# Seven half products in place of eight for the output projection of a hybrid streaming encoder layer

## The chip, the cores and the metric

The kernel runs on one core of a Trainium2 chip. The metric is the device time of one execution in microseconds, as the median of several runs of the same program. Beside the timed runs there is one profiled execution; all rows of the trace come from it. TensorE does the matmuls and writes them to PSUM, VectorE (DVE), ScalarE (ACT) and GpSimd (POOL) do the elementwise work, and SyncE (SP) issues most of the DMAs. GpSimd can't read PSUM.

## What is computed

The layer has 1152 tokens: 1024 of a prompt and 8 times 16 of running streams. It forms a normalised input, one combined input projection of 6664 columns, a matrix-memory branch (mLSTM) and a banded attention branch, and joins them. Only the last part is touched here:

```python
def merge_out(x, h_m, mz, h_a, az, gm, ga, w_bm, w_ba, w_out):
    u_m = jnp.einsum("btc,cd->btd", h_m * jax.nn.silu(mz), w_bm)
    u_a = jnp.einsum("btc,cd->btd", h_a * jax.nn.silu(az), w_ba)
    mix = jax.nn.sigmoid(gm) * u_m + jax.nn.sigmoid(ga) * u_a
    return x + jnp.einsum("btd,de->bte", mix, w_out)
```

Here `h_m` and `h_a` have 512 channels, `mix` and the result 1024. All is float32.

## The kernel before

Everything is held transposed: channels on the 128 partitions, tokens along the columns. A float32 product is made of three fast ones. `split` (L118 to L121) writes a value as a high part (a ScalarE copy to the type fp32r, L120) and a low part (the difference, L121, on VectorE unless GpSimd is named), and `mm3` (L123 to L126) multiplies high by high, high by low and low by high into one PSUM bank. Weights go the same way: a raw tile of 512 columns is loaded (`wr`), and `w_halves` makes `wh` and `wl` of it; `wpA` has three raw buffers and four of each half.

The stages are: input norm; value columns; twelve jobs of the input projection (`chunk_of`, L445 for the matmuls); mLSTM; attention; branch projection of the attention; output projection. The twelve jobs already use a scheme of seven products for eight. There a pair of column tiles is multiplied with sums of quarters of `h` (two halves of the 1024 channels by two halves of the 1152 tokens), which `quarter_sums` (L274 to L289) had formed for 64 tokens at a time, with six VectorE and six GpSimd operations of 4 x 64 columns a call. GpSimd forms the differences of the raw weights (L424).

The last two stages run after the attention, in the function `emit` from L1162 on:

- The last step of the attention writes its outputs to DRAM (`o_sc`), and `load_ops(o_sc, 4)` (L1086) reads them back in pieces of 288 tokens by two tiles and splits them into `h2`. The branch projection of the mLSTM (`um_work`, evacuated at L1098) ran before that, on `h1` and `h21`.
- Branch projection of the attention: eight tiles j, each in three chunks of 384 tokens, 4 x 3 matmuls a chunk. `ev_a` takes a chunk: VectorE multiplies it with the gate (L1174, reads PSUM), GpSimd adds the part of the mLSTM, `sm` (L1175), and `split` writes it to `x_hi` and `x_lo`. `sm` and the gate `ta` come from DRAM, one DMA each of 1152 tokens per j, two sets of buffers.
- Output projection: eight tiles e, each in three chunks of 384 tokens, 8 x 3 matmuls a chunk over the eight tiles of x. The evacuation (L1188) adds the residual x (`xr`, loaded at L1187), and a DMA on ScalarE's queue stores it (L1189).

PSUM has six banks for both stages, taken in turn. The order of the instructions on each engine and queue is fixed when the program is built: a planner simulates the program with costs of its own, and an engine is given the earliest instruction in the text that is ready when it comes free; on the chip each engine then runs that order and waits by semaphores. So loads of the last stage can stand ahead of others (`xr` is issued by SP at 929.8 us). A buffer that lies over one of a closed pool waits until that one has been read for the last time.

Of the kernel before, what the change touches and what calls it, by code (L numbers as in the profile page):

```python
# [32 lines left out]
def emit(tc, a, o, ctx):  # L33
# [4 lines left out]
    def open_pool(name, bufs=1, side=None, space=None):  # L38
        es = ExitStack()
        kw = {"name": name, "bufs": bufs, "reuse_waits": "tile"}  # L40
        if side:
            kw["side"] = side
        if space is not None:
            kw["space"] = space
        return es, es.enter_context(tc.tile_pool(**kw))

    def keep(*args, **kw):
        es, p = open_pool(*args, **kw)
        ctx.enter_context(es)
        return p  # L50
# [54 lines left out]


    h1 = [hp.tile([P, KH, HF], F32R, name=f"h1_{q}") for q in ("hi", "lo")]
    h2 = [hp.tile([P, KH, T], F32R, name=f"h2_{q}") for q in ("hi", "lo")]

    def hcols(k, c0, c1):  # L110

# [1054 lines left out]
    for j in range(8):
        sa = fp.tile([P, 2 * T], F32, tag="sa", name="sa")
        sm, ta = sa[:, 0:T], sa[:, T:2 * T]
        sp.dma_start(sm, sm_sc[j])
        sp.dma_start(ta, tg_sc[8 + j])  # L1170
# [7 lines left out]
        feature_tile(load_nt(a["wba"][j], 4), lambda k, c: hcols(4 + k, c * CH, (c + 1) * CH), ev_a, 4, pp, "pu")  # L1178

    def x_rhs(k, c):  # L1180
        s = slice(c * CH, (c + 1) * CH)
        return x_hi[:, k, s], x_lo[:, k, s]

    for e in range(8):
        def ev(c, ps):
            xr = stg.tile([P, CH], F32, tag="wqr", name="xr", bufs=4).rearrange("p (i t) -> p i t", i=3)
            sp.dma_start(xr, a["xT"][3 * c:3 * c + 3, :, e, :].rearrange("i p t -> p i t"))  # L1187
            dve.scalar_tensor_tensor(out=xr, in0=ps.rearrange("p (i t) -> p i t", i=3), scalar=0.5, in1=xr, op0=ALU.mult, op1=ALU.add)  # L1188
            act.dma_start(o["y"][e][:, c * CH:(c + 1) * CH], xr.rearrange("p i t -> p (i t)"))  # L1189

        feature_tile(load_nt(a["wout"][e]), x_rhs, ev, KD, pp, "pu")
    esPS.close()
    esF.close()

def layout(x):
# [105 lines left out]
```

## Time and profile before

| what | value |
|---|---|
| median of three runs | 1103.8 us (1100.98 to 1110.57) |
| profiled execution | 1099.79 us, its span 1098.0 us |
| TensorE, VectorE, ScalarE, GpSimd busy | 1045.6, 661.7, 529.3, 457.9 us |
| mean granted TensorE clock | 0.989 |
| TensorE's share of the chain that ended last | 62% |

The span runs from the first to the last instruction; the execution has 1.8 us around it. A matmul's recorded duration overlaps with its neighbours', so its price in a dense stretch is the stretch by the number of matmuls. PEld is the loading of weights into TensorE, which overlaps with the matmuls. The branch projection of the attention takes about 937.7 to 992.5 us of the span, the output projection 992.5 to 1094.7.

### The profile page before, as it was taken

What the parts mean: (1) busy time and instruction counts of PE and PEld (TensorE: products, weight loads), DVE (VectorE), ACT (ScalarE), POOL (GpSimd) and SP (SyncE); (2) the same over time, 40 slices, a digit from 0 to 9 for tenths busy, and PEclk for the clock granted to TensorE, in tenths of its full rate; (3) what the DMA queues carried; (4) which work ended last, traced back from release to release, by engine and by line L of the source; (5) the groups of instructions that cost most, each with busy time, mean ns of one, the idle gap of its engine ahead of it and who ended that gap; (6) DMA issues with size and microseconds to landing.
All of it is one profiled execution on the core that took longest, in us unless ns stands there. A gap on an engine that the chain in (4) does not pass through costs nothing.

```text
span 1098.0 us, 22304 instructions
## 1 busy us (share of the span) xinstructions
PE 1045.6 (95%) x8078; PEld 1006.6 (92%) x8078; DVE 661.7 (60%) x1573; ACT 529.3 (48%) x1149; POOL 457.9 (42%) x565
## 2 busy tenths in 40 slices
PE   7989999999998999899999999999996999899998
PEld 5888999999998999899999989989985899799998
DVE  5799335675856554998976555455457467575221
ACT  6633137576768555554432665555566345331110
POOL 3478224363443235544233564564565342352000
PEclk9999999999999999899999999999999999999999
DMA  7432422323322226644537666563564776564432
GB/s 253 169 93 70 119 94 89 119 95 106 106 91 79 91 95 245 212 128 160 172 129 235 209 206 196 183 209 119 183 207 146 220 220 197 175 245 145 133 123 72
DMA packets 126803, 168.45 MB, mean 153 GB/s; under 512 B 14877, under 2 KB 91749, under 8 KB 126182
## 3 DMA queue, kind: packets, MB, share of 16 engines
q1 hardware_dynamic: 118630, 157.60, 44.5%
q10 hardware_dynamic: 8064, 9.44, 2.4%
q8 instruction: 63, 1.03, 0.4%
q14 instruction: 46, 0.38, 0.1%
HBM read 117.03 MB, written 49.96 MB: 152 GB/s over the span
## 4 chain that ended last, share of the span: by engine, by line
PE 62%; DVE 13%; DMA 11%; ACT 4%; issue 4%; POOL 2%; SPq 1%; DVEq 0%; ACTq 0%; POOLq 0%
PE pm L125 10%; PE pm L124 10%; PE pZ L445 10%; PE pm L126 10%; PE pW L445 6%; PE pX L445 6%; DMA raw<-qk_sc 3%; PE pT L817 2%; PE pv L949 2%; DMA raw<-hm_sc 1%; DMA sa<-tg_sc 1%; DMA Mb<-M_sc 1%; PE pS L915 1%; DVE kT L633 1%; PE pS L1002 1%
## 5 line engine op out<-in xcount | busy, mean ns | idle before, releaser
L124 PE MATMUL pm<-h_hi,wh 128*128 128x288 f32 (+1 forms) x864 | 266.4, 309 | 16.9 <-ACT h_hi L120 8.5
L125 PE MATMUL pm<-h_lo,wh 128*128 128x288 f32 (+1 forms) x864 | 265.8, 308 | 1.1 <-DMA h_lo<-h_sc 0.7
L126 PE MATMUL pm<-h_hi,wl 128*128 128x288 f32 (+1 forms) x864 | 263.5, 305 | 0.0
L124 PEld LDWEIGHTS pm<-h_hi,wh 128*128 128x128 f32 x864 | 164.6, 191 | 21.8 <-ACT h_hi L120 10.3
L120 ACT ACTIVATE wh<-wr 128x512 fp32r<-128x512 f32 (+1 forms) x172 | 107.5, 627 | 145.2 <-PE pm L125 89.6
L125 PEld LDWEIGHTS pm<-h_lo,wh 128*128 128x128 f32 x864 | 165.1, 191 | 7.2 <-issue 4.2
L126 PEld LDWEIGHTS pm<-h_hi,wl 128*128 128x128 f32 x864 | 164.8, 191 | 1.5 <-issue 0.8
L121 DVE TENSOR_TENSOR wl<-wr,wh 128x512 fp32r<-128x512 f32 x120 | 88.8, 741 | 41.8 <-ACT wh L120 38.5
L424 POOL TENSOR_TENSOR wr<-wr 128x512 f32<-128x512 f32 x48 | 63.5, 1335 | 73.1 <-DVE wl L121 46.9
L808 POOL TENSOR_SCALAR prob<-prob,mx 128x640 f32<-128x640 f32 (+4 forms) x72 | 51.1, 710 | 98.6 <-DVE mx L807 86.6
L121 POOL TENSOR_TENSOR wl<-wr,wh 128x512 fp32r<-128x512 f32 (+1 forms) x52 | 73.6, 1417 | 31.7 <-ACT wh L120 29.2
L124 PE MATMUL pm<-wh,h_hi 128*128 128x256 f32 (+1 forms) x272 | 78.7, 291 | 3.4 <-ACT h_hi L120 3.4
L126 PE MATMUL pm<-wh,h_lo 128*128 128x256 f32 (+1 forms) x272 | 78.7, 291 | 0.7 <-DVE h_lo L121 0.7
L125 PE MATMUL pm<-wl,h_hi 128*128 128x256 f32 (+1 forms) x272 | 77.9, 288 | 1.4 <-DVE wl L121 1.4
L806 ACT ACTIVATE prob<-prob,mx 128x640 f32<-128x640 f32 (+4 forms) x72 | 51.0, 708 | 41.5 <-DVE mx L805 33.6
L448 DVE TENSOR_TENSOR ring<-pZ,ring 128x288 f32<-128x288 f32 x72 | 32.7, 455 | 59.0 <-PE pZ L445 52.6
L125 PE MATMUL pm<-x_lo,wh 128*128 128x384 f32 x192 | 64.7, 337 | 0.4 <-DVE x_lo L121 0.4
L124 PE MATMUL pm<-x_hi,wh 128*128 128x384 f32 x192 | 64.8, 337 | 0.3 <-ACT x_hi L120 0.3
L126 PE MATMUL pm<-x_hi,wl 128*128 128x384 f32 x192 | 64.7, 337 | 0.0
L458 POOL TENSOR_TENSOR ring<-ring 128x288 f32<-128x288 f32 x24 | 21.7, 904 | 86.2 <-ACT ring L457 83.8
L445 PE MATMUL pW<-S_hi,wh 128*128 128x288 f32 x192 | 56.8, 296 | 0.8 <-ACT ring L457 0.8
L445 PE MATMUL pZ<-S_hi,wh 128*128 128x288 f32 x192 | 56.7, 295 | 0.8 <-DVE ring L448 0.8
(277 smaller groups left out, 2917.2 us busy)
## 6 DMA issues: line engine op xcount, KB each, us to landing
wr<-in_wn SPq DMA_DIRECT2D x88, 256.0 KB
tg_sc<-tg SPq DMA_DIRECT2D x64, 144.0 KB
raw<-qk_sc SPq DMA_DIRECT2D x64, 128.0 KB
kr<-in_Kc SPq DMA_DIRECT2D x16, 512.0 KB
vr<-in_Vc SPq DMA_DIRECT2D x16, 512.0 KB
xt<-in_x SPq DMA_DIRECT2D x9, 512.0 KB
v_sc<-vt SPq DMA_DIRECT2D x72, 64.0 KB
u_sc<-ring SPq DMA_DIRECT2D x32, 144.0 KB
```

Source lines behind the costliest of these rows:

```text
L120: act.activation(out=hi, in_=raw, func=AF.Copy)
L121: eng.tensor_tensor(out=lo, in0=raw, in1=f(hi), op=ALU.subtract)
L124: mm(ps, lhs[0], rhs[0], start=first, stop=False)
L125: mm(ps, lhs[0], rhs[1], start=False, stop=False)
L126: mm(ps, lhs[1], rhs[0], start=False, stop=last)
L424: pool.tensor_tensor(out=out[:, 0:512], in0=x[:, 0:512], in1=y[:, 0:512], op=ALU.subtract)
L445: mm(ps, w[l][:, k, :], x[r][:, k, :], start=first and k + l + r == 0, stop=k == KH - 1 and l == 1, skip_group_check=True)
L448: eng.tensor_tensor(out=out, in0=x, in1=y, op=ALU.add)
L806: act.activation(out=pt[:, :nk], in_=pt[:, :nk], func=AF.Exp, bias=mx[:, 1:2], accum_out=mx[:, 2:3])
L808: pool.tensor_scalar(out=pt[:, :nk], in0=pt[:, :nk], scalar1=mx[:, 3:4], scalar2=1.0, op0=ALU.mult, op1=ALU.mult)
L817: pe.transpose(pT[:, (n - n0) * P:(n - n0 + 1) * P], pt[:, n * P:(n + 1) * P], ident)
L949: mm(pv[:, j * 256:(j + 1) * 256], Vst[p][:, i + 1 - nb + n, j, :], st[:, n].rearrange("p a q -> p (a q)"), start=n == 0, stop=n == nb - 1)
```

## The change

The output projection is done in four pairs of tiles, by seven products of half the channels and half the tokens instead of eight. For that x is no longer held as `x_hi` and `x_lo` of eight tiles, but as seven operands of four tiles by 576 tokens, each with a high and a low part: three quarters of x (`x11`, which takes the place of `h1`, `x12`, `x22`) and four sums of quarters (`S[1]` to `S[4]`). The branch projection forms them. It runs in eight steps, over four jj and two column parts s; a step makes the four chunks of 288 tokens that belong together (tiles jj and jj + 4, both halves of the tokens), with 4 x 3 matmuls each, and then the seven operands. Each is split into a high and a low part. `sm` and `ta` are loaded in pieces of 2 x 288 tokens, two sets of two each.

In `out_pair` the weights of two tiles are loaded in halves of the channels, and four differences of them are formed by GpSimd. Seven products of 4 x 3 matmuls follow, each for s = 0 and s = 1, in three pairs of PSUM banks; four of the results are sums of several products, which VectorE and GpSimd put together from saved copies (`p1`, `p5`, `u2`, `t_`).

The pool of `h2` moves to the other side of SBUF, so that it can be closed after the branch projection. A new pool `end`, in part over its place, holds half of the raw and split weights of the output projection, `xr` and the saved copies. `xT` gets a layout in which a tile's tokens are contiguous.

```diff
-    x_hi = fp.tile([P, KD, T], F32R, name="x_hi", bufs=1)
-    x_lo = fp.tile([P, KD, T], F32R, name="x_lo", bufs=1)
...
-        def ev_a(c, ps):
-            s = slice(c * CH, (c + 1) * CH)
-            dve.scalar_tensor_tensor(out=ta[:, s], in0=ta[:, s], scalar=1.0, in1=ps, op0=ALU.add, op1=ALU.mult)
-            pool.tensor_tensor(out=sm[:, s], in0=sm[:, s], in1=ta[:, s], op=ALU.add)
-            split(x_hi[:, j, s], x_lo[:, j, s], sm[:, s])
...
+    for jj in range(KH):
+        w = [load_nt(a["wba"][jj + KH * e], 4) for e in range(2)]
+        for s in range(2):
+            c = slice(s * HC, (s + 1) * HC)
...
+            for e in range(2):
+                for half in range(2):
+                    ps = pp.tile([P, 512], F32, tag=banks[count % 6], name="pu")[:, :HC]
+                    count += 1
+                    for k in range(KH):
+                        mm3(ps, w[e][k], hcols(KH + k, half * HF + s * HC, half * HF + (s + 1) * HC), k == 0, k == KH - 1)
+                    x, t_ = sm[e][:, half, :], ta[e][:, half, :]
+                    dve.scalar_tensor_tensor(out=t_, in0=t_, scalar=1.0, in1=ps, op0=ALU.add, op1=ALU.mult)
+                    pool.tensor_tensor(out=x, in0=x, in1=t_, op=ALU.add)
...
+            put(x11, r11)
+            put(x12, r12)
+            dve.tensor_tensor(out=t1, in0=r21, in1=r22, op=ALU.add)
+            put(S[1], t1)
+            dve.tensor_tensor(out=t2, in0=t1, in1=r11, op=ALU.subtract)
+            put(S[2], t2)
+            pool.tensor_tensor(out=t4, in0=r12, in1=t2, op=ALU.subtract)
+            put(S[4], t4)
+            dve.tensor_tensor(out=t3, in0=r11, in1=r21, op=ALU.subtract)
+            put(S[3], t3)
+            put(x22, r22, pool)
+    esA.close()
+    esH2.close()
+    esE, ep = open_pool("end", side="right")
+    turns = {"wr": [wpA] * 3 + [ep] * 4, "wh": [wpA] * 4 + [ep] * 3, "wl": [wpA] * 4 + [ep] * 3}
...
+        def out(e, half, s, x):
+            n, c = (n1, n2)[e], slice(half * HF + s * HC, half * HF + (s + 1) * HC)
+            xr = ep.tile([P, HC], F32, tag="xr", name="xr", bufs=6)
+            sp.dma_start(xr, a["xT"][n][:, c])
+            dve.scalar_tensor_tensor(out=xr, in0=x, scalar=0.5, in1=xr, op0=ALU.mult, op1=ALU.add)
+            act.dma_start(o["y"][n][:, c], xr)
...
+        b11, b21 = load(n1, 0), load(n1, 1)
+        w[1] = halves(b11)
+        w[2] = halves(b21)
+        b12, b22 = load(n2, 0), load(n2, 1)
+        sub(b11, b12, b11)
+        w[5] = halves(b11)
+        t2 = w_raw()
+        sub(t2, b22, b11)
+        w[6] = halves(t2)
+        w[3] = halves(b22)
+        sub(b12, b22, b12)
+        w[7] = halves(b12)
+        sub(b21, b21, t2)
+        w[4] = halves(b21)
...
+        for s in both:
+            product(X[s], w[1], part(x11, s), True)
+            act.activation(out=p1[s], in_=X[s], func=AF.Copy)
+        for s in both:
+            product(X[s], w[2], part(x12, s), False)
+            out(0, 0, s, X[s])
+        for s in both:
+            product(W[s], w[5], part(S[1], s), True)
+            act.activation(out=p5[s], in_=W[s], func=AF.Copy)
+            pool.tensor_tensor(out=t_[s], in0=p1[s], in1=p5[s], op=ALU.add)
+        for s in both:
+            product(Z[s], w[6], part(S[2], s), True)
+            add(dve, u2[s], Z[s], p1[s])
+        for s in both:
+            product(W[s], w[3], part(S[4], s), False)
+            add(dve, u2[s], W[s], u2[s])
+            out(1, 0, s, u2[s])
+        for s in both:
+            product(Z[s], w[7], part(S[3], s), False)
+            add(dve, t_[s], Z[s], t_[s])
+            out(1, 1, s, t_[s])
+        for s in both:
+            product(Z[s], w[4], part(x22, s), False)
+            add(dve, p1[s], Z[s], p1[s])
+            out(0, 1, s, p1[s])
+
+    for n1 in range(0, 8, 2):
+        out_pair(n1, n1 + 1)
```

## Rows read from the trace of the kernel before

**Rows 1.** The page: each engine's busy time, share and instructions.

```profile
PE 1045.6 (95%) x8078; PEld 1006.6 (92%) x8078; DVE 661.7 (60%) x1573; ACT 529.3 (48%) x1149; POOL 457.9 (42%) x565
```

**Rows 2.** Busy time (instructions) in stretches around the last two stages.

```profile
core 0: us, PE busy (x) PEld busy (x) DVE busy (x) ACT busy (x) POOL busy (x), PEclk, DMA share, GB/s
940.00:950.00 10.00, 7.58 (x33) 7.01 (x32) 2.27 (x3) 2.05 (x3) 0.74 (x2) 0.83 0.76 243
950.00:960.00 10.00, 10.00 (x60) 10.00 (x59) 7.97 (x12) 3.61 (x7) 6.75 (x6) 1.00 0.40 140
990.00:1000.00 10.00, 9.33 (x52) 8.75 (x52) 7.97 (x12) 4.13 (x8) 6.21 (x6) 1.00 0.39 139
1000.00:1050.00 50.00, 50.00 (x287) 50.00 (x286) 12.91 (x22) 5.06 (x8) 0.00 (x0) 1.00 0.44 143
```

**Rows 3.** Three operations on x: durations in ns (min/median/max), first and last start.

```profile
L1174 DVE SCALAR_TENSOR_TENSOR sa<-sa,pm x24: 539/547/555, 950.9 to 997.3; 128x384 f32<-128x384 f32 x24
L1175 POOL TENSOR_TENSOR sa<-sa x24: 1006/1214/1463, 951.5 to 997.9; 128x384 f32<-128x384 f32 x24
L121 DVE TENSOR_TENSOR x_lo<-sa,x_hi x24: 543/793/1368, 953.5 to 999.7; 128x384 fp32r<-128x384 f32 x24
```

**Rows 4.** Timeline (start, us): seam of the two stages, and the last matmul.

```profile
992.29 0.34 PE L126 MATMUL pm<-h_hi,wl 128*128 128x384 f32 x1
992.46 0.33 PE L124 MATMUL pm<-x_hi,wh 128*128 128x384 f32 x1
...
1094.33 0.33 PE L126 MATMUL pm<-x_hi,wl 128*128 128x384 f32 x1
1094.70 0.56 DVE L1188 SCALAR_TENSOR_TENSOR xr<-pm,xr 128x384 f32<-128x384 f32 x1 [3.64 <-PE pm L126]
```

**Rows 5.** Stretches of the input projection: its first job, and all twelve.

```profile
146.00:166.00 20.00, 20.00 (x154) 20.00 (x153) 7.36 (x13) 8.49 (x17) 6.55 (x6) 1.00 0.29 94
143.00:427.00 284.00, 280.99 (x2117) 280.08 (x2116) 167.59 (x336) 180.28 (x383) 115.00 (x109) 1.00 0.31 101
```

**Rows 6.** Timeline of VectorE and of GpSimd, 986 to 988.5 us.

```profile
986.07 0.68 DVE L121 TENSOR_TENSOR wl<-wr,wh 128x512 fp32r<-128x512 f32 x1
986.67 1.37 DVE L121 TENSOR_TENSOR x_lo<-sa,x_hi 128x384 fp32r<-128x384 f32 x1
988.21 0.56 DVE L121 TENSOR_TENSOR x_lo<-sa,x_hi 128x384 fp32r<-128x384 f32 x1 [0.17 <-ACT x_hi L120]
...
986.22 1.40 POOL L1175 TENSOR_TENSOR sa<-sa 128x384 f32<-128x384 f32 x1 [0.96 <-DVE sa L1174]
```

**Rows 7.** Sums of `quarter_sums`, a 288-wide GpSimd addition (ns), raw weights' differences (page).

```profile
L280 DVE TENSOR_TENSOR sx<-h_hi,h_lo x18: 405/951/961, 50.3 to 104.4; 128x256 f32<-128x256 f32 x18
L280 POOL TENSOR_TENSOR sx<-h_hi,h_lo x18: 730/908/1069, 51.9 to 106.8; 128x256 f32<-128x256 f32 x18
L458 POOL TENSOR_TENSOR ring<-ring x24: 801/814/1156, 149.5 to 415.8; 128x288 f32<-128x288 f32 x24
L424 POOL TENSOR_TENSOR wr<-wr 128x512 f32<-128x512 f32 x48 | 63.5, 1335 | 73.1 <-DVE wl L121 46.9
```

**Rows 8.** The nine calls of `quarter_sums`: the stretch, and weights converted in it.

```profile
51.80:110.50 58.70, 51.63 (x411) 50.03 (x410) 55.37 (x106) 21.17 (x53) 46.59 (x54) 0.97 0.30 99
L121 DVE TENSOR_TENSOR wl<-wr,wh 128x512 fp32r<-128x512 f32 x8 | 7.5, 951 | 0.0
```

**Rows 9.** Timeline of the attention's end and the first loads after it.

```profile
932.31 0.46 DVE L1098 SCALAR_TENSOR_TENSOR tm<-tm,pm 128x288 f32<-128x288 f32 x1 [1.05 <-PE pm L126]
939.30 0.88 SPq L1086 DMA_DIRECT2D raw<-o_sc  x2
942.21 0.68 ACT L120 ACTIVATE h_hi<-raw 128x576 fp32r<-128x576 f32 x1 [3.71 <-DMA raw<-o_sc]
942.93 1.64 DVE L121 TENSOR_TENSOR h_lo<-raw,h_hi 128x576 fp32r<-128x576 f32 x2 [3.71 <-ACT h_hi L120]
943.82 0.40 SPq L1169 DMA_DIRECT2D sa<-sm_sc  x1
```

More of the change, by code (lines that the diff above doesn't have):

```diff
@@ L107, in emit @@
     h1 = [hp.tile([P, KH, HF], F32R, name=f"h1_{q}") for q in ("hi", "lo")]
-    h2 = [hp.tile([P, KH, T], F32R, name=f"h2_{q}") for q in ("hi", "lo")]
+    esH2, hp2 = open_pool("h2", side="right")
+    h2 = [hp2.tile([P, KH, T], F32R, name=f"h2_{q}") for q in ("hi", "lo")]
     def hcols(k, c0, c1):
@@ L785, in emit @@
     turns = {t_: [wpA] for t_ in turns}
-    stg = keep("stage", bufs=2, side="left")
+    esStg, stg = open_pool("stage", bufs=2, side="left")
     esB, bp_ = open_pool("attnP", bufs=2, side="right")
@@ L1159, in emit @@
     esH.close()
-    esF, fp = open_pool("fin", bufs=2, side="right")
-    esPS, pp = open_pool("pF", bufs=6, space=PSUM)
-    x_hi = fp.tile([P, KD, T], F32R, name="x_hi", bufs=1)
-    x_lo = fp.tile([P, KD, T], F32R, name="x_lo", bufs=1)
[L1166 to L1170, printed above, removed]
-        def ev_a(c, ps):
-            s = slice(c * CH, (c + 1) * CH)
-            dve.scalar_tensor_tensor(out=ta[:, s], in0=ta[:, s], scalar=1.0, in1=ps, op0=ALU.add, op1=ALU.mult)
-            pool.tensor_tensor(out=sm[:, s], in0=sm[:, s], in1=ta[:, s], op=ALU.add)
-            split(x_hi[:, j, s], x_lo[:, j, s], sm[:, s])
-        feature_tile(load_nt(a["wba"][j], 4), lambda k, c: hcols(4 + k, c * CH, (c + 1) * CH), ev_a, 4, pp, "pu")
@@ L1180, in x_rhs @@
[L1180 to L1191, printed above, removed]
+    esStg.close()
@@ new lines, in emit, with put @@
+    esF, fp = open_pool("fin", side="left")
+    esA, sap = open_pool("sa", bufs=4, side="right")
+    esPS, pp = open_pool("pF", space=PSUM)
+    x11 = h1
+    x12, x22, S[1], S[2], S[3], S[4] = ([fp.tile([P, KH, HF], F32R, name=f"{n_}_{q}") for q in ("hi", "lo")]
+                                        for n_ in ("x12", "x22", "X1", "X2", "X3", "X4"))
+    banks = [f"b{q}" for q in range(6)]
+    count = 0
+    for jj in range(KH):
+        w = [load_nt(a["wba"][jj + KH * e], 4) for e in range(2)]
+        for s in range(2):
+            c = slice(s * HC, (s + 1) * HC)
+            sm, ta = ([sap.tile([P, 2, HC], F32, tag=t_, name=t_) for _ in range(2)] for t_ in ("sm", "ta"))
+            for e in range(2):
+                for t_, src in ((sm, sm_sc[jj + KH * e]), (ta, tg_sc[8 + jj + KH * e])):
+                    sp.dma_start(t_[e], src.rearrange("p (h t) -> p h t", h=2)[:, :, c])
+            for e in range(2):
+                for half in range(2):
[6 more added lines that the diff above has]
+                    pool.tensor_tensor(out=x, in0=x, in1=t_, op=ALU.add)
+            r11, r21, r12, r22 = sm[0][:, 0, :], sm[0][:, 1, :], sm[1][:, 0, :], sm[1][:, 1, :]
+            t1, t2, t3, t4 = ta[0][:, 0, :], ta[0][:, 1, :], ta[1][:, 0, :], ta[1][:, 1, :]
+            def put(q, raw, eng=dve):
+                split(q[0][:, jj, c], q[1][:, jj, c], raw, eng)
+            put(x11, r11)
[9 more added lines that the diff above has]
+            put(x22, r22, pool)
@@ L1192, in emit @@
+    for n1 in range(0, 8, 2):
+        out_pair(n1, n1 + 1)
     esPS.close()
+    esE.close()
     esF.close()
@@ L1204, in layout @@
     xa = np.concatenate([x["x_prompt"][0], x["x_sample"].reshape(P, 1024)], 0)
-    d["xT"] = c(xa.reshape(NT, P, KD, P).transpose(0, 3, 2, 1))
+    d["xT"] = c(xa.T).reshape(KD, P, T)
     w = x["w_in"][0].reshape(KD, P, 6664).transpose(1, 0, 2)
```

16 lines of the change are left out of this document (added).

## The prediction, made before the changed kernel was run

> **What bounds the kernel now.** I read the page first: TensorE is busy 1045.6 of 1098.0 us [rows 1], so a change that takes matmuls away can pay, if nothing else becomes late in the stretch that it touches. Next, the busy time in stretches [rows 2]: from 950 us on TensorE is busy in all of each stretch but about the one at 990. Before that, at 940 to 950, it waits for the attention's last results, and there the granted clock is 0.83 as a mean, that is, the lower of its two levels (1.2 GHz) for 3.4 us; it had stood idle just before. VectorE is busy 8.0 and GpSimd 6.8 of 10 us while the branch projection runs, and fall to a quarter and to nothing in the output projection. The timeline at the seam shows the first matmul on x_hi at 992.5 and the last at 1094.3 us [rows 4]: the output projection follows the branch projection with no gap, and x is finished only just in time. So the end is TensorE's, but the two other engines stand close behind it in the branch projection.
>
> **The output projection's matmuls.** Removed: 8 tiles by 3 chunks by 8 k by 3 = 576 matmuls of 384 columns. 287 of them fill 50 us [rows 2], 0.174 us each: 100.3 us. Added: 4 pairs by 7 products by 2 column parts by 12 = 672 of 288 columns. The same `product` ran in the first job of the input projection: 154 matmuls in 20 us [rows 5], 0.130 each: 87.3 us. The term is -13.0 us. Over all twelve jobs a matmul took 284/2117 = 0.134 us [rows 5]; the 0.0042 more, by 168 matmuls of a pair, is 0.7 us for each pair's waits on weights and banks, for four pairs +2.9 us. I take all of it, since the last job's weight preparation (7 conversions and 4 subtractions a pair) is the same here; 0 is the other end.
>
> **The branch projection's matmuls.** 288 of 384 columns (50.1 us) become 384 of 288 (49.9 us): nothing.
>
> **The sums behind the branch projection**, in eight steps (one jj, one s). Before, an x piece cost VectorE one merge from PSUM and one subtraction, and GpSimd one addition; over the stage 24, 24 and 24, all 384 wide [rows 3]. Now each step costs VectorE 4 merges, 3 sums and 6 subtractions, GpSimd 4 additions, one subtraction for t4 and one for x22, and one weight subtraction, all but that 288 wide. What matters is that VectorE's subtraction and GpSimd's addition do not run beside each other. At 986.2 a GpSimd addition began; VectorE's x_lo, issued at 986.67, took 1.37 us, and ended about 0.4 after the addition, where the x_lo at 988.2, with GpSimd still, took 0.56 [rows 6]. The merges, which read PSUM, keep 0.54 to 0.56, whatever runs beside them [rows 3]. So two-input work from SBUF on both engines adds up as if on one.
> The price of a step on that shared way: for VectorE 288 wide lies between 0.405 (256 wide) and 0.543 (384 wide) [rows 7], by a straight line 0.44, nine times 3.96; for GpSimd 0.80 [rows 7], six times 4.80; the weight 0.68 [rows 6]. Sum 9.44 us, against 48 matmuls of 0.130 = 6.2 us on TensorE. That TensorE could hide it is thus excluded unless the two engines overlap more than these rows show.
> A lower bound comes from the nearest thing to such a step in this kernel, `quarter_sums`: nine calls of 6 VectorE and 6 GpSimd operations of 256 columns. Their shortest durations, 9 x (6 x 0.405 + 6 x 0.730) = 61.3, and 8 weights x 0.68 = 5.4, make 66.7 us, and all of it was done in 58.7 [rows 7, 8], a share of 0.88, because the recorded ends overlap. That gives 8.3 us a step. I take the middle, 8.9: the new step has a longer chain from one operation to the next than `quarter_sums`, and only two sets of buffers, so I don't expect the full packing.
> The Trainium skill ("SBUF — State Buffer", Who interferes with whom) says that a VectorE instruction with two SBUF inputs contends with a GpSimd instruction that reads SBUF, and that the loser blocks fully. By that rule taken strictly the step costs the whole 9.44 and the forecast below would be 3.8 us later; by the pace of rows 8 it would be 4.1 earlier.
>
> **When the output projection can start.** Each product sums over four k, and these are the four jj, so the first product on s = 1 needs x11 of the eighth step. In the kernel before, the sum over eight k could begin while the last tile was still being formed; this cover is gone. The first step can't finish before the later quarters of h are split: 942.93 + 1.64 = 944.6 [rows 9]. Its two sums and two subtractions on the first quarter, 2 x 0.80 + 2 x 0.44 = 2.5 us, can be done before. Seven steps: 944.6 - 2.5 + 7 x 8.9 = 1004.4. The head of the eighth: merge 0.46 [rows 9], addition 0.80, copy 0.5 and subtraction 0.44, and one addition in between, 0.8: 1007.4. The first product (12 x 0.130 = 1.6 us, s = 0) runs before that: start 1005.8. Now the start that corresponds is 1094.7 - 100.3 = 994.4 [rows 4]. The term is +11.4 us; its ends are +7.3 (8.3 a step) and +15.2 (9.44), and 3 us either way for the first step's start.
>
> **What waits then.** TensorE stands idle for some us ahead of the products; after the idle time near 942 it lost 3.4 us x 1/2 = 1.7 us of work at the lower clock [rows 2]. I put +1.7, between 0 and 3.4. The rest of the eighth step (5 x 0.44 + 2 x 0.80 = 3.8 us) and the first pair's preparation (subtractions of 1.3 and conversions of 0.68) share one queue on VectorE and GpSimd: b11, w5, t2 and w6 need 4.0, together 7.8, where w6 is wanted 6 x 1.6 = 9.6 us after the start. But b22 and t2 lie in a pool over h2, so their load is issued after the last branch matmul, and a load takes about 2.9 us here (raw, 939.30 to 942.2 [rows 9]). I put +2, between 0 and 8 (the whole 7.8 late).
>
> **Moved and small edits, together.** The sm and ta loads go from 16 of 576 KB to 32 of 288 KB, the same bytes; SP issues one in 0.4 us, beside. They lie over h21, last read before 932.3, instead of over the attention's buffers, so they need not wait until 943.8 as now [rows 9]: that is why step one is set by h and not by them. xr goes from 24 loads of 192 KB to 32 of 144 KB, the stores likewise, the stores on ScalarE's queue, which is busy 5 of 50 us there [rows 2]; GpSimd issues no DMA. xr can no longer be fetched ahead, since its pool lies over h2 and the sum buffers; the first result waits for it, while TensorE goes on in other banks: nothing. h2 on the other side of SBUF changes no instruction. In the output projection a pair costs VectorE 7 conversions of 0.68 and 16 operations of 0.46, 12 us, GpSimd 4 subtractions of 1.3 [rows 7] and 2 additions of 0.80, 7 us, beside 22 us of matmuls: hidden. The tail has one VectorE addition more: 0.46.
>
> **Sum.** -13.0 + 2.9 + 11.4 + 1.7 + 2 + 0.4 = +5.4 us. The profiled execution, 1099.8 us, would become 1105.2. It lies 4.0 below the median of the three runs, 1103.8; on the median's scale the forecast is **1109.2 us**, half a per cent up. Its ends: 5.4 - 4.1 - 3 - 1.7 - 2 = -5.4, and 5.4 + 3.8 + 3 + 1.7 + 6 = +19.9.
>
> **Rivals.**
> (a) *The first pair comes late*, slower by over 1%. The eighth step's remains and the first pair's weights queue behind each other on the shared way, at the strict price: from w5 on TensorE waits, 8 instead of 2 us, and the steps cost 9.44: 5.4 + 3.8 + 6 = +15.2, 1119.0 us. It decides once the preparation of w6 ends later than 9.6 us after the first product. For it: VectorE's order has the sums ahead of the weights. Against: two of the seven weights need no subtraction and their buffers come free a jj earlier.
> (b) *TensorE stays the bound*: the early start of the sums (12 us ahead of the present one, 950.9 [rows 3], at the best) and slack on VectorE hide the steps. Then -13.0 - 0.2 + 0.4 = -12.8, and 0 to 2.9 for the pairs: -11.4, 1092.4 us. For it: the merges run free of GpSimd, and TensorE has six banks to run ahead. Against: 9.44 or 8.3 us of work in a step of 6.2, eight times.
> (c) *The change doesn't do what it says*: a matmul of 288 columns costs as much as one of 384, and 672 outnumber 576. Rows 5 speak against it: 0.130 against 0.174.
>
> **Chances.** The forecast's case 0.56, of which 0.12 ends over 1% slower; (a) 0.26; (b) 0.16, of which 0.11 over 1% faster; (c) 0.02. One per cent, 11 us, is about what a measurement of this kernel tells from no change. So faster 0.11, within 1% 0.51, slower 0.38. The range takes the forecast's ends, widened down to most of (b) and cut at +19: 1094 to 1123; the forecast's own range is 1098 to 1124.
>
> **What would show it.** Right: an L445 matmul spacing near 0.13 in the last stage; over the branch projection TensorE with gaps and VectorE with GpSimd near full, x11 pieces some 8.9 us apart; a gap of several us ahead of the first product, and the lower clock near it. Wrong: TensorE gapless to the end, with GpSimd's 288-wide additions at 0.80 and VectorE's subtractions at 0.44 throughout (then b); or a second gap of over 4 us inside the first pair (then a).

## The result, and the profile after

The changed kernel is 0.7% slower: 1114.2 us (median of 17 runs, 1107.5 to 1121.1) against 1105.1 (17 runs, 1101.0 to 1110.6), ratio **1.0074**, 95% interval 1.0054 to 1.0093. The ratio, worked out over all these runs, makes +8.2 us; the two medians by themselves lie 9.1 us apart. The forecast was half a per cent, +5.4 us, with the case "within 1%" as the likeliest.

The profiled execution took 1118.9 us. Its attention ends 10 us later than in the profile of before, 948.6 against 938.5 us (start of VectorE's last `pvs`). In the kernels below it fell anywhere from 936.4 to 948.8, and both ends are of kernels (2 and 5) whose edits to the changed kernel lie behind that point. So this shift is between executions and not of the change. I therefore compare stages from this point on, **the last evacuation** (kernels 9 to 12 need a correction, given there). First the stretch from there to TensorE's last matmul, before and after (us, then each engine's busy time and instructions, granted clock, DMA):

```profile
938.50:1094.70 156.20, 153.07 (x861) 151.60 (x859) 62.23 (x95) 26.34 (x47) 29.51 (x27) 0.99 0.45 150
```

```profile
948.60:1113.10 164.50, 148.07 (x1054) 145.10 (x1052) 120.10 (x202) 50.58 (x107) 77.98 (x75) 0.95 0.47 140
```

The stretch grew by 8.3 us, as much as the ratio makes. TensorE is busy 5.0 us less, and idle 16.4 instead of 3.1 us. VectorE's busy time has doubled (62 to 120 us), and GpSimd's more than doubled. The next view, after, answers to [rows 2]:

```profile
950.00:960.00 10.00, 5.58 (x34) 5.34 (x34) 1.83 (x3) 1.70 (x3) 1.64 (x3) 0.83 0.55 163
960.00:970.00 10.00, 10.00 (x66) 10.00 (x65) 8.94 (x16) 4.62 (x10) 6.69 (x7) 0.83 0.08 15
970.00:980.00 10.00, 10.00 (x78) 10.00 (x77) 9.66 (x18) 3.17 (x8) 6.74 (x7) 1.00 0.66 194
980.00:990.00 10.00, 9.89 (x75) 9.65 (x74) 9.66 (x18) 4.44 (x10) 6.66 (x7) 1.00 0.62 180
990.00:1000.00 10.00, 8.36 (x59) 7.60 (x57) 9.67 (x19) 4.55 (x11) 6.42 (x7) 1.00 0.66 191
1000.00:1010.00 10.00, 8.15 (x58) 7.71 (x59) 10.00 (x15) 3.45 (x9) 8.48 (x9) 1.00 0.44 120
1010.00:1020.00 10.00, 3.64 (x21) 2.82 (x19) 9.68 (x18) 4.65 (x12) 6.91 (x9) 0.90 0.43 119
1020.00:1030.00 10.00, 9.59 (x57) 9.58 (x58) 7.59 (x14) 4.69 (x12) 5.98 (x7) 0.76 0.24 76
1050.00:1100.00 50.00, 50.00 (x380) 50.00 (x379) 29.37 (x51) 11.59 (x22) 15.72 (x13) 1.00 0.49 146
```

Read it down the columns. VectorE is 97% busy from 970 to 1020, while TensorE, full until 990, loses more and more. A mean clock of 0.83 over 10 us is a loss of 1.7 us of work; the rows at 950, 960, 1010 and 1020 lose 1.7 + 1.7 + 1.0 + 2.4 = 6.8 us at most, since TensorE stands idle in a part of them. In short windows, with busy time alone, the whole stretch loses 6.2, where before only the 1.7 of [rows 2] was lost. The account of the 8.3 us is then: 13.3 more idle, 4.5 more at the lower clock (1.2 GHz), and 9.5 less work at the full clock (5.0 + 4.5). The last row gives the price of a matmul in the output projection: 50/380 = 0.132 us for 288 columns, as against 50/287 = 0.174 for 384 [rows 2].

Two stops of TensorE make most of the idle time, and short ones stand in between and behind. These are matmuls with a wait in front of them, in TensorE's timeline after (start, duration, wait and releaser in brackets):

```profile
957.71 0.61 PE L125 MATMUL pu<-h_hi,wh 128*128 128x288 f32 x1 [4.42 <-ACT h_hi L121]
...
1005.54 0.40 PE L125 MATMUL pu<-h_hi,wh 128*128 128x288 f32 x1 [1.76 <-DVE ta L1188]
1011.52 0.40 PE L125 MATMUL pu<-h_hi,wh 128*128 128x288 f32 x1 [0.97 <-DVE ta L1188]
1017.89 0.52 PE L446 MATMUL py<-X_hi,wh 128*128 128x288 f32 x1 [4.52 <-ACT wh L121]
1020.41 0.61 PE L446 MATMUL py<-X_hi,wl 128*128 128x288 f32 x1 [1.28 <-DVE wl L122]
1046.87 0.40 PE L446 MATMUL py<-x_hi,wh 128*128 128x288 f32 x1 [1.65 <-DVE tt L449]
```

The first stop waits for pieces of `h`, the second stands ahead of the first product. What ends the second is a weight's high half, and on ScalarE this stands behind the copies of the steps, one of which waits 2.6 us for an addition on GpSimd:

```profile
1015.07 0.44 ACT L121 ACTIVATE x_hi<-sm 128x288 fp32r<-128x288 f32 x1 [2.61 <-POOL sm L1189]
...
1017.23 0.61 ACT L121 ACTIVATE wh<-wr 128x512 fp32r<-128x512 f32 x1
```

So the first product, too, waits for the work behind the branch projection. In between, the merges on VectorE (`ta`, L1188) free the PSUM banks late. After each long stop the clock is at the lower level: the rows at 950 and 960 lose up to 3.4 us together, and so do those at 1010 and 1020.

**Where the first stop comes from.** SP's queue after:

```profile
936.70 0.32 SPq L967 DMA_DIRECT2D o_sc<-ot  x1
941.83 0.58 SPq L1180 DMA_DIRECT2D sm<-sm_sc  x1
...
946.45 0.65 SPq L1180 DMA_DIRECT2D ta<-tg_sc  x1
947.20 1.35 SPq L567 DMA_DIRECT2D wr<-in_wba  x1
948.67 0.35 SPq L967 DMA_DIRECT2D o_sc<-ot  x1
953.86 0.37 SPq L1087 DMA_DIRECT2D raw<-o_sc  x1
954.64 0.33 SPq L967 DMA_DIRECT2D o_sc<-ot  x1
955.02 0.43 SPq L1087 DMA_DIRECT2D raw<-o_sc  x1
```

Eight loads for the first two steps stand ahead of the attention's last stores. The first of them waits until 941.8 for the mLSTM's branch projection, whose operands lay in that place, and the eight take 5.3 us to issue. Only then comes the store at 948.67; the reload at 953.86 has to wait for its landing, and the last store behind it waits too. Before, those loads came behind `h` (943.82 [rows 9]). Store and reload also lie further apart: 5.2 us, where it was 3.1 (936.22 to 939.30); what makes the landing longer was not tested. The last low part of `h` begins 12.3 us after the last evacuation, where it was 8.3 (the first two lines are of before, the third of after):

```profile
936.22 0.34 SPq L966 DMA_DIRECT2D o_sc<-ot  x1
946.82 0.76 DVE L121 TENSOR_TENSOR h_lo<-raw,h_hi 128x576 fp32r<-128x576 f32 x1 [2.26 <-ACT h_hi L120]
960.91 0.76 DVE L122 TENSOR_TENSOR h_lo<-raw,h_hi 128x576 fp32r<-128x576 f32 x1 [0.40 <-ACT h_hi L121]
```

It is 11.9 to 13.1 us in all seven kernels in which the eight loads stand there and whose last evacuation has no other work in front (changed, 1, 2, 3, 5, 7, 8).

**The two engines in a step.** Durations after (ns, min/median/max), to hold against [rows 3, 7], and two neighbouring stretches of their timelines:

```profile
L1189 POOL TENSOR_TENSOR sm<-sm,ta x32: 788/958/1257, 951.0 to 1023.0; 128x288 f32<-128x288 f32 x32
L122 DVE TENSOR_TENSOR X_lo<-ta,X_hi x32: 443/770/1077, 965.6 to 1027.8; 128x288 fp32r<-128x288 f32 x32
L1188 DVE SCALAR_TENSOR_TENSOR ta<-ta,pu x32: 440/442/455, 950.4 to 1022.4; 128x288 f32<-128x288 f32 x32
L122 DVE TENSOR_TENSOR h_lo<-sm,h_hi x8: 446/876/1514, 960.1 to 1021.2; 128x288 fp32r<-128x288 f32 x8
```

```profile
1011.03 0.44 DVE L1188 SCALAR_TENSOR_TENSOR ta<-ta,pu 128x288 f32<-128x288 f32 x1
1011.39 0.91 DVE L122 TENSOR_TENSOR X_lo<-ta,X_hi 128x288 fp32r<-128x288 f32 x1
1012.22 1.06 DVE L122 TENSOR_TENSOR h_lo<-sm,h_hi 128x288 fp32r<-128x288 f32 x1
1013.21 0.44 DVE L122 TENSOR_TENSOR X_lo<-ta,X_hi 128x288 fp32r<-128x288 f32 x1
```

```profile
1011.18 0.80 POOL L1202 TENSOR_TENSOR ta<-sm,ta 128x288 f32<-128x288 f32 x1 [0.76 <-DVE ta L1200]
1011.94 1.03 POOL L1189 TENSOR_TENSOR sm<-sm,ta 128x288 f32<-128x288 f32 x1
```

A VectorE subtraction that begins while GpSimd adds (1011.39, 1012.22) ends some 0.3 us after GpSimd's operation does, and the next one, with GpSimd still, takes 0.44. The merges read PSUM and keep 0.44 throughout. The low parts of x11 (`h_lo<-sm`, one a step) begin (1021.2 - 960.1)/7 = 8.7 us apart, where 48 matmuls take 6.3. Over these seven steps VectorE is busy 58.8 of 61.2 us, with 91 operations of the steps, seven weight conversions and two pieces of `h`:

```profile
960.07:1021.25 61.18, 50.81 (x349) 48.56 (x349) 58.80 (x100) 25.16 (x57) 42.91 (x44) 0.95 0.47 134
```

As an estimate from these rows: nine operations with two SBUF inputs at 0.37 us from start to start, six of GpSimd at 0.80 and a weight at 0.6, in a row, are 8.7 us, if the four merges find room beside GpSimd.

### The profile page after: what moved, and what is told of

Read it like the earlier page. It is cut to its first block, busy times and chain, and to the rows that moved or that the text cites. A ratio compares the mean times of both kernels' runs of the same rounds, so it can differ in the third digit from the quotient of the medians.

```text
span 1117.2 us, 23013 instructions
## 1 busy us (share of the span) xinstructions
PE 1045.0 (94%) x8270; PEld 1003.2 (90%) x8270; DVE 719.6 (64%) x1681; ACT 553.4 (50%) x1209; POOL 505.8 (45%) x613
## 3 DMA queue, kind: packets, MB, share of 16 engines
q10 hardware_dynamic: 9216, 9.44, 2.5%
## 4 chain that ended last, share of the span: by engine, by line
PE 60%; DVE 12%; DMA 11%; issue 5%; ACT 4%; POOL 3%; SPq 2%; POOLq 0%; ACTq 0%; DVEq 0%
PE pZ L446 9%; PE pm L125 7%; PE pm L126 6%; PE pm L127 6%; PE pW L446 6%; PE pX L446 6%; PE py L446 6%; DMA raw<-qk_sc 3%; PE pT L818 2%; DMA u<-u_sc 2%; PE pv L950 1%; DMA vraw<-v_sc 1%; DVE kT L634 1%; DMA raw<-hm_sc 1%; DVE qT L634 1%
## 5 line engine op out<-in xcount | busy, mean ns | idle before, releaser
L125 PE MATMUL pm<-h_hi,wh 128*128 128x288 f32 x768 | 234.0, 305 | 15.7 <-ACT tg L585 6.5
L126 PE MATMUL pm<-h_lo,wh 128*128 128x288 f32 x768 | 233.5, 304 | 1.7 <-DMA h_lo<-h_sc 0.9
L127 PE MATMUL pm<-h_hi,wl 128*128 128x288 f32 x768 | 231.2, 301 | 0.0
L125 PEld LDWEIGHTS pm<-h_hi,wh 128*128 128x128 f32 x768 | 146.8, 191 | 19.8 <-ACT h_hi L121 7.1
L126 PEld LDWEIGHTS pm<-h_lo,wh 128*128 128x128 f32 x768 | 147.4, 192 | 7.7 <-issue 4.2
L127 PEld LDWEIGHTS pm<-h_hi,wl 128*128 128x128 f32 x768 | 147.2, 192 | 1.5 <-issue 0.8
L122 DVE TENSOR_TENSOR wl<-wr,wh 128x512 fp32r<-128x512 f32 x132 | 102.9, 783 | 36.4 <-ACT wh L121 32.8
L446 PE MATMUL pX<-h_hi,wh 128*128 128x288 f32 x192 | 56.7, 296 | 0.5 <-ACT ring L456 0.5
L446 PE MATMUL pW<-S_hi,wl 128*128 128x288 f32 x192 | 56.6, 295 | 0.0
L446 PE MATMUL pX<-h_lo,wh 128*128 128x288 f32 x192 | 56.6, 295 | 0.0
```

The source lines that it names most:

```text
L125: mm(ps, lhs[0], rhs[0], start=first, stop=False)
L126: mm(ps, lhs[0], rhs[1], start=False, stop=False)
L127: mm(ps, lhs[1], rhs[0], start=False, stop=last)
L446: mm(ps, w[l][:, k, :], x[r][:, k, :], start=first and k + l + r == 0, stop=k == KH - 1 and l == 1, skip_group_check=True)
```

## The experiments

Each row gives the ratio to the kernel before, then the pace of the low parts of x11, and the time from the last evacuation to the first matmul of the output projection and to the last, all in us from the profiled execution. Beside these kernels' runs the kernel before had medians between 1100.5 and 1105.1.

| kernel | ratio (95%) | pace | to first | to last |
|---|---|---|---|---|
| before | 1 | - | 53.9 | 155.8 |
| changed | 1.0074 (1.0054 to 1.0093) | 8.74 | 69.3 | 164.2 |
| 1 all sums on VectorE | 1.0065 (1.0040 to 1.0089) | 8.81 | 66.1 | 164.3 |
| 2 four additions on VectorE | 1.0056 (1.0036 to 1.0077) | 8.67 | 65.8 | 163.1 |
| 3 without the additions | 0.9974 (0.9952 to 0.9996) | 7.12 | 60.2 | 154.0 |
| 4 first two steps' loads after h | 1.0105 (1.0076 to 1.0135) | 8.60 | 69.3 | 166.0 |
| 5 without additions and sums | 0.9926 (0.9897 to 0.9955) | 6.42 | 57.7 | 148.2 |
| 6 second step's loads after h | 1.0043 (1.0019 to 1.0067) | 8.66 | 66.0 | 160.2 |
| 7 = 2, merges first | 1.0058 (1.0034 to 1.0082) | 8.80 | 66.4 | 163.5 |
| 8 products between steps | 1.0105 (1.0071 to 1.0139) | - | - | 170.6 |
| 9 = 8, weights early | 1.0036 (1.0015 to 1.0057) | - | - | 158.9 |
| 10 = 9, second loads after h | 1.0057 (1.0033 to 1.0082) | - | - | 161.0 |
| 11 = 10, additions on VectorE | 1.0009 (0.9987 to 1.0030) | - | - | 157.1 |
| 12 = 11, loads as they were | 1.0027 (1.0006 to 1.0048) | - | - | 157.9 |

**1 and 2: is it the two engines' excluding each other, or the amount of work?** Kernel 1 moves all six of GpSimd's operations of a step to VectorE, kernel 2 only the four additions (the first edit).

```diff
-                    pool.tensor_tensor(out=x, in0=x, in1=t_, op=ALU.add)
+                    dve.tensor_tensor(out=x, in0=x, in1=t_, op=ALU.add)
...
-            pool.tensor_tensor(out=t4, in0=r12, in1=t2, op=ALU.subtract)
+            dve.tensor_tensor(out=t4, in0=r12, in1=t2, op=ALU.subtract)
...
-            put(x22, r22, pool)
+            put(x22, r22)
```

> The changed kernel, but the six GpSimd operations of a step (four additions, t4, the low part of x22) are given to VectorE. Theory A (two-input work from SBUF on VectorE and GpSimd runs as if on one engine, and that sets the 8.7 us of a step): one on VectorE costs 0.37 us from start to start where it cost 0.75 on GpSimd, so a step is 19 x 0.37 + 0.6 = 7.6 us, the x11 pieces come 7.6 apart, 7 x 1.1 = 8 us are won: ratio to the kernel before about 1.000. Theory B (the engines run side by side; chain and loads set the step): VectorE gets 40% more work and nothing is relieved: the step stays at 8.7 or grows, ratio 1.007 to 1.012. Theory C (the loss is h's late arrival behind the early loads on SP): no change, 1.007.

> The changed kernel with only the four additions of a step moved to VectorE; t4 and x22's low part stay on GpSimd, where they can run beside the four merges from PSUM. Theory A: the shared way holds 13 x 0.37 + 0.6 + 2 x 0.75 = 6.9 us, VectorE itself 17 x 0.37 + 0.6 = 6.9: steps of about 7.0 to 7.4, 9 to 12 us won, ratio 0.996 to 1.000. Theory B: as slow as or slower than the changed kernel, 1.007 to 1.010. Theory C: 1.007.

Both missed theory A's gain: the pace hardly moved. Kernel 1's ratio and pace are what theories B and C had said. The contention did go, as kernel 1's durations show:

```profile
L122 DVE TENSOR_TENSOR X_lo<-ta,X_hi x32: 445/452/459, 954.8 to 1015.5; 128x288 fp32r<-128x288 f32 x32
949.13:1010.83 61.70, 52.15 (x365) 50.92 (x365) 56.19 (x146) 25.04 (x57) 6.45 (x1) 0.94 0.46 133
```

But 19 operations a step now stand on one engine, 0.37 us from start to start: 7.0 us, and a weight of 0.6. With two pieces of `h` and some operations of the step that follows, which fall into this stretch, 8.0 of the 8.8 us of a step are VectorE's own (56.2 of 61.7 us in the second line). The rest are waits, for `ta` loads above all. So the steps take as long on one engine as on the two; that they come out alike is in part chance, since the operations moved are cheaper on VectorE, and the waits, which its sum had left out, took the gain. With that, theory A is no longer that the exclusion costs the time, but that the amount of work does, as the expectations from kernel 5 on put it. Kernel 1 has one more row that shows the exclusion, a GpSimd weight subtraction that takes 1.3 us elsewhere [rows 7], between VectorE operations that follow each other without a gap:

```profile
985.88 6.45 POOL L1224 TENSOR_TENSOR wr<-wr 128x512 f32<-128x512 f32 x1 [46.53 <-DVE wl L122]
...
990.38 0.82 DVE L122 TENSOR_TENSOR X_lo<-ta,X_hi 128x288 fp32r<-128x288 f32 x2
991.36 0.82 DVE L1188 SCALAR_TENSOR_TENSOR ta<-ta,pu 128x288 f32<-128x288 f32 x2 [0.16 <-DMA ta<-tg_sc]
992.10 0.55 DVE L1202 TENSOR_TENSOR ta<-sm,ta 128x288 f32<-128x288 f32 x1
```

It ended at 992.33, once two merges from PSUM had left it the way. The Trainium skill ("SBUF — State Buffer", Who interferes with whom) says that the two engines contend for a shared pair of ports, which is an exclusive lock, and that a VectorE instruction with at most one input in SBUF, outside the modes that use both ports, does not contend; the 6.45 us and the merges' constant 0.44 agree. In kernels 2 and 7 a 288-wide GpSimd subtraction (`t4`) is held in the same way, 3.35 us, at 980.86 and 983.04.

**3 and 5: less work.** Kernel 3 leaves the four additions of `sm` out, kernel 5 also the four sums of quarters (that is eight operations a step; its expectation says seven).

```diff
-                    dve.scalar_tensor_tensor(out=t_, in0=t_, scalar=1.0, in1=ps, op0=ALU.add, op1=ALU.mult)
-                    pool.tensor_tensor(out=x, in0=x, in1=t_, op=ALU.add)
+                    dve.scalar_tensor_tensor(out=x, in0=t_, scalar=1.0, in1=ps, op0=ALU.add, op1=ALU.mult)
...
-            dve.tensor_tensor(out=t1, in0=r21, in1=r22, op=ALU.add)
-            put(S[1], t1)
...
+            put(S[1], r21)
```

> The changed kernel without the four GpSimd additions of a step: the mLSTM part is loaded but not added, the merge writes the value itself (this part of the result is left out). Theory A: shared way 9 x 0.37 + 0.6 + 2 x 0.75 = 5.4 us, under TensorE's 6.3: x11 pieces 6.4 apart, 7 x 2.3 + 1 = 17 us won, ratio 0.992, and what is left shows the gain of the seven products. Theory B: the chain gets shorter by one addition, once, 1 to 2 us: 1.006. Theory C: 1.007, at most 2 us less.

> Leaves out the four additions of sm in every step and the four sums of quarters (the operands S[1] to S[4] are split from single quarters), so seven of a step's 17 two-input operations on SBUF are gone and seven products remain. Theory A (VectorE's work, stretched by GpSimd's operations, sets the pace of a step): ten VectorE operations of about 0.37 us are 3.7 us and one GpSimd operation 0.75 us, less than TensorE's 6.2 us for 48 matmuls, so the low parts of x11 come 6.2 to 6.6 us apart (8.74 in the changed kernel, 7.12 without the additions alone), the first product comes 50 to 55 us after the attention's last evacuation, and the ratio to the kernel before is 0.985 to 0.992. Rival B (the loads of sm and ta through two sets of buffers set the pace): they are all still there, so the pace stays at 7.1 or more and the ratio above 0.995.

Kernel 3's pace came down to 7.12, but missed the 6.4, and its ratio the 0.992. The 5.4 us expected for its shared way had left out the merges, which are VectorE's too: its 13 operations at 0.37, a weight of 0.6 and two of GpSimd's at 0.80 in a row are 7.0, as an estimate. Kernel 5's pace is what theory A said; its ratio, 0.9926, is a hair above the range, and its first product, at 57.7 us, came later than the 50 to 55. Rival B (loads through two buffer sets) is refuted. The seven steps of kernel 5 between the first and the last low part of x11, and the stretch behind them:

```profile
958.10:1003.01 44.91, 44.91 (x322) 44.91 (x322) 34.27 (x80) 24.33 (x58) 7.96 (x8) 0.94 0.66 189
1003.00:1010.00 7.00, 7.00 (x55) 7.00 (x54) 4.34 (x10) 3.36 (x8) 0.80 (x1) 1.00 0.37 112
```

TensorE is full in the steps and runs into the first product (1006.6) with no stop, though the loads and buffers are all still there; VectorE is busy 76% of the steps, where it was 96%. This is what seven products are worth where their operands cost nothing: 155.8 - 148.2 = 7.6 us, with a late `h` still in it. The additions and sums take 164.2 - 148.2 = 16 us of the changed kernel.

**4 and 6: the late h.** Kernel 4 ties all eight loads of the first two steps behind the last piece of `h`, kernel 6 only the second step's four, by a one-column copy on GpSimd into the load's buffer (shown is kernel 6; kernel 4 has `if jj == 0`).

```diff
+                    if (jj, s) == (0, 1):
+                        pool.tensor_copy(out=t_[e][:, 0, 0:1], in_=f(h2[0][:, 3, T - 1:T]))
                     sp.dma_start(t_[e], src.rearrange("p (h t) -> p h t", h=2)[:, :, c])
```

> The changed kernel, but the eight loads of sm and ta for the first two steps wait until the last piece of h has been read back (a GpSimd copy of one column ties them to it), as they did in the kernel before. Theory C: the last pieces of h arrive 9 us after the attention's last evacuation instead of 13 to 14, the start of the steps moves by 4 to 5 us, and with it the end: ratio 1.003. Theory A: the steps keep 8.7 us, and their start moves less, since the first sm and ta now arrive later: 0 to 4 us won, ratio 1.004 to 1.007.

> Ties only the second step's loads of sm and ta (four of the eight that stand ahead of the attention's last stores on SP's queue) behind the last piece of h; the first step's stay where they are. Theory C (four us of the loss come from h being late by SP's order): h's last low part comes 9 to 10 us after the attention's last evacuation (12.3 in the changed kernel), the first step is not delayed, the time from that evacuation to the end falls from 164 to about 161 us, ratio 1.003 to 1.005. Rival: what h gains the second step loses by its late loads, as when all eight were tied (ratio 1.0105): ratio 1.006 to 1.011.

In kernel 4 `h` came 5 us sooner (7.3 after the last evacuation), but the loads began only at 944.85, 8 us after it, and the first low part of x11 ended 16.2 us after it instead of 11.9: a new wait in place of the old one, and no test of the theory. Kernel 6 is the test, and it came out as theory C said: `h` at 9.5 (9.3 in kernels 10 and 11, which have the same tie), the first x11 earlier by 2.7 us, 160.2 us to the end, ratio 1.0043. The ratio alone would not carry it, since its interval overlaps that of the changed kernel. Its SP queue, where only four loads precede the store:

```profile
936.89 0.59 SPq L1182 DMA_DIRECT2D sm<-sm_sc  x1
...
938.88 0.61 SPq L1182 DMA_DIRECT2D ta<-tg_sc  x1
939.59 0.54 SPq L567 DMA_DIRECT2D wr<-in_wba  x1
940.81 0.33 SPq L967 DMA_DIRECT2D o_sc<-ot  x1
```

**7: the order of the merges.** On kernel 2, where TensorE stood 5.3 us at 985 for a merge, the operands of a step are written behind the next step's merges.

```diff
+            def operands(jj=jj, c=c, sm=sm, ta=ta):
...
+            if late:
+                late.pop()()
+            late.append(operands)
+    late.pop()()
```

> The kernel with the additions on VectorE (ratio 1.0056), and the seven operands of a step written behind the four merges of the step after, so that no merge stands behind sums. Theory O (PSUM banks come free late because merges queue behind sums; TensorE then stands, 5.4 us at 985 in that kernel, and its clock falls): the gap goes, the first product comes 3 to 5 us earlier, ratio 1.000 to 1.003. Theory A (VectorE's whole work sets the pace): TensorE only waits elsewhere, low parts of x11 still 8.5 to 8.8 us apart, ratio 1.004 to 1.007. Theory B (two sets of sm and ta): sets are held for longer, so loads come later, pace above 9 us, ratio over 1.008.

As theory A: 1.0058, pace 8.80. The stop did not go; it is 6.3 us at 986 in kernel 7. Where VectorE has no time left, the order only chooses what waits.

**8 to 12: giving TensorE something to do.** All steps of s = 0 run first, then those of s = 1; three products of the first pair for s = 0, 36 matmuls, are put between the last steps. The branch weights are held for both s in columns of x and h2 that are free at the time, the later stages have fewer spare buffers, and the branch projection takes five PSUM banks in turn in place of six.

```diff
-    for jj in range(KH):
...
-        for s in range(2):
+    for s in range(2):
+        for jj in range(KH):
+            if s == 0:
+                wb[jj] = [branch_weights(jj, e) for e in range(2)]
...
+            if s and jj == 2:
+                X0 = bank(0, 0)
+                product(X0, w0[0][1], part(x11, 0), True)
```

> The changed kernel with the steps in another order, first the four of s = 0, then the four of s = 1, and three products of the first output pair (w1 x11, w5 S1, w6 S2, each for s = 0, 36 matmuls of 0.131 us, 4.7 us) put between the last steps, where TensorE stands by theory A. Their weights and the branch weights of jj = 0 and 1 lie in columns of h2 and x that are free then. Theory A: TensorE has about 10 us to spare in the last four steps, so the 4.7 us cost nothing there, the wait of 4.7 us before the first product goes as well, and half of its low clock: time from the attention's last evacuation to the end 164 to about 155 to 159 us, ratio 0.998 to 1.003. Rival: three of the first pair's weight conversions now compete with the steps on VectorE and push the steps out by as much (3 to 5 us): ratio 1.004 to 1.008.

Missed, and above the rival's range too: 1.0105. TensorE stood 13.7 us before the first step (949.91) for the first weights, which the order put behind `h` on ScalarE:

```profile
949.91 0.61 PE L125 MATMUL pu<-h_hi,x_hi 128*128 128x288 f32 x1 [13.67 <-ACT x_hi L121]
```

Kernel 9 keeps the first two jj's weights in their old buffers, and holds those of jj = 2 and 3 instead.

```diff
-        if jj >= 2:
+        if jj < 2:
             return load_nt(a["wba"][jj + KH * e], 4)
...
-        for jj in range(KH):
+        for jj in (2, 3, 0, 1) if s else range(KH):
```

> As the kernel with three products between the steps, but the branch weights of the first two jj are in their old buffers and those of jj = 2 and 3 in the free columns of x, since there TensorE waited 13.7 us for the first weights. From the first low part of x11 to the end that kernel took 147.6 us, the changed kernel 152.6. Theory A: with the wait gone the first low part of x11 comes 12 us after the attention's last evacuation as in the changed kernel, so from that evacuation to the end about 159 to 160 us (164.2 in the changed kernel), ratio 1.002 to 1.005. Rival: the 5 us were gained because TensorE's wait let VectorE's queue and the weights run ahead; then 163 to 165 us, ratio 1.006 to 1.009.

The time, 158.9 us, and the ratio, 1.0036, are as theory A said, but not the first low part of x11, which comes 1.5 us after the last evacuation and not 12. In this order the first step begins before the attention has ended, and on VectorE its first merge stands ahead of the last evacuation and waits for its `ta`:

```profile
945.30 0.46 DVE L1253 SCALAR_TENSOR_TENSOR ta<-ta,pu 128x288 f32<-128x288 f32 x1 [3.01 <-DMA ta<-tg_sc]
945.67 0.68 DVE L961 TENSOR_TENSOR pvs<-pv,pvs 64x512 f32<-64x512 f32 x1
```

So the last evacuation itself is late in kernels 9 and 12, and in 9 to 12 fewer matmuls stand behind it (1016 to 1033, against 1054). A mark that all of them share is the last merge of the mLSTM's branch projection (L1099), with 1081 matmuls behind it in each:

```profile
941.83:1113.10 171.27, 152.62 (x1081) 149.23 (x1079) 123.62 (x209) 53.91 (x114) 79.34 (x78) 0.95 0.49 144
936.96:1104.90 167.94, 152.54 (x1081) 150.12 (x1079) 122.55 (x209) 53.24 (x114) 78.03 (x78) 0.94 0.50 147
```

From it to the end the changed kernel takes 171.3 us, kernel 9 167.9, 10 168.0, 11 164.0 and 12 167.1; the kernel before takes 162.4. So kernel 9 wins back 3.3 of the 8.9 us lost, and as much of TensorE's idle time is gone (18.7 us in the first line, 15.4 in the second): a part of the loss is idle time that other work can fill. Kernel 10 adds the edit of kernel 6 (for the step that is second here), kernel 11 that of kernel 2, kernel 12 takes kernel 6's edit out again.

> The same, with the second step's loads of sm and ta tied behind the last piece of h, which by itself took the ratio from 1.0074 to 1.0043. If the two costs (late h, TensorE standing in the steps) are separate, they add up: 155 to 157 us from the attention's last evacuation to the end (155.8 in the kernel before), ratio 0.998 to 1.002. If not, it is no better than the better of the two, 1.003 to 1.005.

> The same again, with the four additions on VectorE, which by itself was worth 1 us or so (1.0074 to 1.0056). Additive: 154 to 156 us from the attention's last evacuation to the end, ratio 0.996 to 1.001, so at best level with the kernel before. Rival: with TensorE's waits already filled, VectorE's longer queue delays the merges and the products between the steps, ratio 1.002 or more.

> As the last kernel (ratio 1.0009, 157.1 us from the attention's last evacuation to the end), but the second step's loads of sm and ta stay ahead of the attention's last stores. Of the 36 products between the steps, eight now come behind the last step, where TensorE stood 5.4 us. If the two moves (products between steps, additions on VectorE) carry the gain: ratio 0.998 to 1.001, 156 to 158 us. If the tie is what made the difference between 1.0036 and 1.0009: ratio 1.002 to 1.005, 159 us or more.

Kernel 10 did not add up: its time by the shared mark is kernel 9's, and its ratio is above the 1.003 to 1.005 of the other case too. Kernel 11's ratio is in the additive range and its 157.1 us just above it. The four additions on VectorE gained here what they had not gained in kernel 2: 1.0057 to 1.0009, with intervals that do not overlap, and 4.0 us by the shared mark. Kernel 12's ratio, 1.0027, and its 167.1 us speak for the tie, its 157.9 us from the late last evacuation for the other case; but by their ratios 9 and 10, and 11 and 12, differ within their intervals and in opposite directions, so what the tied loads are worth in this order stays open. Kernel 11 is the best of those that do the whole computation: 1.0009 (0.9987 to 1.0030), level with the kernel before, not better. The same stretch of kernel 11, from its last evacuation on:

```profile
943.90:1101.30 157.40, 144.30 (x1033) 140.96 (x1031) 113.49 (x234) 50.45 (x107) 52.51 (x47) 0.97 0.50 146
```

TensorE still stands 13 of the 157 us; 5.2 of them come ahead of the first product of s = 1.

## Why the prediction was right, and by how much not

The sign, the size class and the mechanism held: the sums behind the branch projection take longer than its matmuls, and that eats the seven products' gain. By its terms:

- **Output projection's matmuls and pairs, -13.0 + 2.9.** The added matmuls were put at 87.3 + 2.9 = 90.2 us; from the first of them on TensorE is busy 89.5 us, counted at the full clock: 0.133 us a matmul, between the 0.130 and 0.134 of the two views in [rows 5]. Rival (c) fell.
- **Branch projection's matmuls, 0.** Where nothing holds them up, 78 fill 10 us (row 970), 0.128 each, so this stands; as the steps' pace isn't TensorE's, it hardly counts.
- **A step, 8.9 us (8.3 to 9.44).** 8.7. That the amount of work on VectorE and GpSimd sets the pace is shown by kernel 5 (6.4, TensorE's own, with loads and buffers as they were) and by VectorE's busy share, 96% in the changed kernel and 91% in kernel 1. What falls is a part of the picture: taking the exclusion alone away is worth little, since VectorE by itself has too much. Rival (b) needed a step that hides in 6.2 us, and fell with the 8.7 of the changed kernel itself.
- **Start of the products, +11.4.** By the working the first product begins 67.3 us after the last evacuation (1005.8 - 938.5); it began after 69.3. The seven steps between first and eighth cost 61.2 us in place of 62.3, and the first product began 3.8 us before the eighth low part of x11 was ready, in place of 1.6. But the first step failed: "The first step can't finish before the later quarters of h are split: 942.93 + 1.64 = 944.6", with 3 us either way. By that working the first low part of x11 ended 1007.4 - 62.3 = 945.1, 6.6 us after the last evacuation; it ended 11.9 after it, 5.3 later. The step was set by `h`, as said, but `h` does not keep its time. The prediction had seen that the loads of `sm` and `ta` "need not wait until 943.8", entered this as a help, and put their issue at 0.4 us each, "beside". Each took 0.6, and on SP's in-order queue the eight came ahead of the attention's last stores and put `h` off by 4.0 us. Kernel 6, with half of them out of the way, got 4.0 of the 8.4 us back to the end of the kernel.
- **Clock, +1.7.** +4.5: there is a second stop of over 4 us, the one for `h`, and each is followed by its own stretch at the lower level; 2.8 us of the loss lie behind the first product. This and the late `h` are the two terms that were too small.
- **The first pair, +2 (0 to 8).** Waits of 1.3 and 1.7 us are seen in it and at its end, 2.9 together. Rival (a) asked for a second stop of over 4 us there; there is none, so it fell too.
- **The small moves and the tail** show no wait in the timeline of the output projection beyond these.

From the first product on, the working has 90.2 + 2 + 1.7 + 0.4 = 94.3 us; it took 89.5 + 2.9 + 2.8 = 95.2. So 2.0 us of the forecast's error lie ahead of the first product and 0.9 behind it, together the 3 us between +5.4 and +8.2. That it is no more is in part luck: ahead of the first product 5.3 us too little for the first step met 3.3 too much for what came after it.

## What to carry to other kernels

Before counting the matmuls that such a scheme saves, add up the VectorE and GpSimd operations with two SBUF inputs behind them as if one engine did them all, and hold the sum against TensorE's time for the same piece, and so all of VectorE's own operations, those that read PSUM with them; if a sum is larger, leaving operations out or giving TensorE other work helps. Moving operations between the two engines did next to nothing by itself (kernels 1 and 2), and 0.5% once TensorE had other work (10 to 11). A load that can be issued earlier is not free: look at what stands behind it on the same queue, and whether that feeds the next stage. Of a stop of TensorE, count its length and the lower clock after it.

## What the runs showed of the hardware that was not expected

- A GpSimd operation can be held off for as long as VectorE runs two-input operations from SBUF without a gap: 6.45 us for one that takes 1.3 (kernel 1), 3.35 for one that takes 0.80 (kernels 2 and 7).
- VectorE's 288-wide operations follow each other at 0.37 us, recorded as 0.45; the prediction's 0.44 a piece was too dear. GpSimd's additions have a median of 0.96 beside them, where it took 0.80; that includes the time in which they are held off, so recorded durations of the two engines can't simply be added.
